# A decoder block with a mixture of experts: the two single pairs gathered row by row, filler products in the waits, and the closing stage written into both arms of the overflow branch

## The chip, the cores and the metric

The kernel runs on one core of a Trainium2 chip. The metric is the device time of one execution in microseconds (us), lower is better. The program is written by hand for five engines: TensorE (PE, matrix products, with its weight loads as PEld), VectorE (DVE), ScalarE (ACT), GpSimd (POOL) and SyncE (SP), whose queue here issues every transfer between the main memory and the on-chip memory SBUF. Products land in PSUM, which has eight banks of 128 x 512 float32.

## The reference

One layer on 512 tokens of width 1024, in float32: a first half (conditioned norm, one input projection, differential attention, a diagonal state-space branch, a gated merge) that leaves the residual `x`, and then a mixture of experts, which this document is about. Cut to its core, as the kernel computes it:

```python
h = modulate(rms_norm(x, norm2_g), shift2, scale2)            # 512 x 1024
grp = argmax(h @ w_rg + b_rg)                                  # one of 4 groups
top_v, top_i = top_k((h @ w_re + b_re)[grp], 2)                # 2 of the 8 experts in it
comb = p_grp * softmax(top_v)
for each token t and each of its two experts e:                # 32 experts in all
    a, g = split(h[t] @ w_e_in[e], 2)                          # 1024 -> 2 x 512
    moe[t] += comb * ((silu(a) * g) @ w_e_out[e])              # 512 -> 1024
x = x + gate2 * moe
y = rms_norm(x, final_g)
```

## The kernel before

The 32 experts are worked off as 16 pairs, p = 0 to 15 (`NP` = 16). An expert has 64 places (`CAP`), a pair has 128, so that one pair fills the 128 partitions. Four tiles of 128 tokens (`NT` = 4) feed the pairs. A token's row is brought to its place by a product with a selection matrix `P` (128 tokens by 128 places, a single 1 per chosen token; `P0` is that of pair 0, made during the routing). The normed input is kept as the sum of two tiles, `mh` + `ml`, so every such product is done twice.

For each pair, in order: `gather` (products at L1155) gives the transposed input `xT`, 1024 x 128, as eight blocks: for block k, tile i and half w the stationary operand is a 128 x 128 block of `mh` or `ml`, the moving one is `P`. Pairs are gathered two at a time (256 moving columns), except pair 0, gathered during the routing by `stage_x` (`x_` in the table `beside`), and pair 15, gathered alone when pair 13 is worked: both with 128 moving columns, 64 products each. Then `places` (L1341) finds token numbers and weights of the places, `hid_mm` (L1393) multiplies `xT` with `w_e_in` (tile `hid`), `act` and `act_turn` make and transpose the activated tile (`sa`, `xtp`, L1301), `yb_mm` (L1400) multiplies with `w_e_out` (tile `yb`), `weigh` weights it and splits it in two again (`yf`, `yh`, `yl`), and `give` (L1378) takes the rows back to the tokens with the transposed selection `PT` (tile `cb`), and adds them to `x` on DVE. `give` of pair p - 1 is done inside the pass of pair p.

The weights, 12 slots of 1 MB to a pair, stream through a ring of 17 slots. SP's queue issues them in order (`fetch`, L1263); each issue waits until the slot's last reader is done. The orders of PE and SP are written by hand in this part; DVE and ACT are ordered by a scheduler until pair 15's second half, and by hand from there on.

Ahead of the pairs stands the last product of the first half (`po`, L185), and between its steps the routing of the four token tiles, placed by the table `beside`: `t_` transposes, `l_` makes the logits (L1088) and ranks them on DVE, `h_` makes `mh` and `ml`, `r_` counts the places (L1137) and makes `P0` for one tile, `x_` gathers pair 0. After the last `po` of tile 3, step (3, 15), the rest of the routing has PE to itself.

At the end, after pair 15's first product, a register `ov` tells whether an expert got more than 64 tokens. Only then does `overflow` run, a long loop. The closing stage follows: pair 15's second product in five column pieces (`yq`, L1555), their way back to the tokens, and the final norm. In it GpSimd multiplies the left halves of `x` with `final_g` into the output tiles `fo`. In the profiled execution `overflow` did not run.

DVE's helpers have one line each for all their uses: L90 (`tt`, two tensors), L93 (`ts`), L96 (`stt`).

Of the kernel before, what the change touches and what calls it, by code (L numbers as in the profile page):

```python
# [19 lines left out]
T, D = 512, 1024  # L20
# [37 lines left out]
def hybrid_block(ctx: ExitStack, tc: tile.TileContext, x, cols, cst, ada_a, ada_b, b_rows, bc_rows, lamv, relb,  # L58
# [1098 lines left out]

    def weights():
# [49 lines left out]
    t_, l_, r_, h_, x_ = stage_t, stage_l, stage_r, stage_h, stage_x  # L1208
# [5 lines left out]
              (3, 15): [(x_, 1), (l_, 3, T, 256), (t_, 3, 768, 256), (r_, 2), (l_, 3, 768, 256), (h_, 3), (x_, 2), (r_, 3),  # L1214
                        (x_, 3)]}
    with tc.manual_schedule(engines={mybir.EngineType.PE}):
# [10 lines left out]
        for i in range(NT):  # L1227
# [11 lines left out]
            if i == 0:  # L1239
                xg0 = [bank(4 + q, (128, 4, 128), name="xg") for q in range(2)]  # L1240
# [81 lines left out]
    def gather(ps, P, h, between=None):  # L1322
# [121 lines left out]
    ctx.enter_context(tc.manual_schedule(engines={mybir.EngineType.SP, mybir.EngineType.PE}))  # L1444
    gate2 = per.tile([128, D], F32, tag="gate2", name="gate2")
# [6 lines left out]
    for h in range(2):  # L1452
        halves(x_half(0, h), xg0[h])
    for p in range(NP - 1):
# [73 lines left out]
    pl = [bank(4 + j, name="cb") for j in range(2)]  # L1528
    for j in range(2):
        give_mm(NP - 2, ys[1], 2 + j, pl[j])  # L1530
# [5 lines left out]
    for j in range(2):  # L1536
        add(2 + j, 512, pl[j])
# [5 lines left out]
    PIECES = ((0, 256), (256, 256), (512, 256), (768, 128), (896, 128))  # L1543
    fo = [slot("fo", free[0] + (3, 5, 8, 9)[i]) for i in range(NT)]
    yfs, yhl = slot("yf", free[0] + 6), slot("y", free[0] + 7, F32R)
    yp, ys, wide = {}, {}, {}
    nxf = nx.rearrange("p a b -> p (a b)")
    v4, y4, t4 = (nxf[:, 20 + 4 * j:24 + 4 * j] for j in range(3))

    def piece(q):  # L1550
        c0, n = PIECES[q]
        yp[q] = bank(q % 2, name="yq")[:, :n]
        for f in range(4):
            for e in range(2):
                TE.matmul(yp[q][64 * e:64 * e + 64], hT_[:, f, 64 * e:64 * e + 64], ring[NP - 1][8 + q][:, e, f],  # L1555
                          start=f == 0, stop=f == 3, skip_group_check=True)
        ys[q] = [yfs[:, 0, c0:c0 + n]]
        stt(ys[q][0], yp[q], disp[NP - 1][0][:, 6:7], gate2[:, c0:c0 + n], OP.mult, OP.mult)
        if q < 3:
            ys[q] += [yhl[:, j, c0:c0 + n] for j in range(2)]  # L1560
            S.copy(ys[q][1], ys[q][0])

    def second_part(q):
        yf, yh, yl = ys[q]
        tt(yl, yf, f32(yh), OP.subtract)
        ys[q] = [yh, yl]

    def to_tokens(qs_, i):
        for q in qs_:
            c0, n = PIECES[q]  # L1570
            if q < 2 and i == 0:
                wide[q] = pair(name="cb").rearrange("p a (b c) -> p (a b) c", c=256)
            elif q == 2:
                wide[2, i] = bank(4 + i, name="cb")
            give_mm(NP - 1, ys[q], i, wide[q][:, i] if q < 2 else wide[2, i][:, c0 - 512:c0 - 512 + n])

    def add_square(q, i):
        add(i, 256 * q, wide[q][:, i] if q < 2 else wide[2, i])
        square(q, i)

    def square(q, i):
        cs = slice(256 * q, 256 * q + (256 if q < 2 else 512))
        S.activation(fo[i][:, 1, cs], xs[i][:, cs], AF.Square, accum_out=nxf[:, 4 * q + i:4 * q + i + 1])

    def root(i):
        S.activation(t4[:, i:i + 1], nxf[:, 8 + i:9 + i], AF.Sqrt, bias=v4[:, i:i + 1], scale=1.0 / D)

    def inverse(i):

        v, y, t = (a[:, i:i + 1] for a in (v4, y4, t4))  # L1590
        emit(y, lambda: V.reciprocal(y, t))  # L1591
        stt(v, nxf[:, 8 + i:9 + i], 1.0 / D, v, OP.mult, OP.add)
        stt(t, y, -0.5, v, OP.mult, OP.mult)
        tt(t, t, y, OP.mult)
        stt(y, t, 1.5, y, OP.add, OP.mult)

    def finish(i):
        r_ = y4[:, i:i + 1]
        S.activation(fo[i][:, 0, :512], fo[i][:, 0, :512], AF.Copy, scale=r_)
        stt(fo[i][:, 0, 512:], xs[i][:, 512:], r_, fg[1], OP.mult, OP.mult)  # L1600
        nc.sync.dma_start(out[128 * i:128 * i + 128, :], fo[i][:, 0])

    def in_turns(*fs):
        for _ in in_steps([fs]):
            pass


    S.activation(t4[:, 0:1], eps6, AF.Sqrt)
    piece(0)
    second_part(0)  # L1610
    piece(1)
    for i in range(NT):
        to_tokens((0, ), i)
    for i in range(NT):
        add(i, 0, wide[0][:, i])
        if i == 1:
            second_part(1)
    for i in range(NT):
        square(0, i)
    piece(2)  # L1620
    for i in range(NT):
        to_tokens((1, ), i)
    for i in range(NT):
        add(i, 256, wide[1][:, i])
        if i == 0:
            second_part(2)
    for i in range(NT):
        square(1, i)
        tt(fo[i][:, 0, :512], xs[i][:, :512], fg[0], OP.mult, eng=G)
    piece(3)  # L1630
    piece(4)
    for i in range(NT):
        to_tokens((2, 3, 4), i)
        if i == 0:
            ts(v4, nxf[:, 0:4], 1.0 / D, OP.mult, 1e-6, OP.add)
            stt(v4, nxf[:, 4:8], 1.0 / D, v4, OP.mult, OP.add)
            add_square(2, 0)
            root(0)
        elif i < 3:
# [136 lines left out]
```

## Time and profile before

| what | value |
|---|---|
| median of 3 runs | 954.73 us (953.29 to 957.48) |
| the profiled execution | 954.63 us, of which its trace spans 952.5 us |
| PE busy | 909.0 us, 95% of the span |
| DVE, ACT, POOL busy | 501.5, 298.2, 7.2 us |
| mean granted clock of TensorE | 0.968 of full speed |
| weights and other transfers | 268.68 MB, mean 282 GB/s |

The profile's busy time of PE is no proof that PE does useful work at its full speed: products overlap, their ends are modelled, and the granted clock has two levels, 2.4 GHz (1.00 in the rows) and 1.2 GHz (0.50). The 2.1 us between the span and the execution's time lie outside the trace.

### The profile page before, as it was taken

How to read it: one execution, taken by the hardware profiler on the slowest of the kernel's cores; microseconds unless marked ns; L12 is line 12 of the kernel's file. 1: busy time of each engine (PE TensorE's matmuls, PEld its weight loads, DVE VectorE, ACT ScalarE, POOL GpSimd, SP SyncE). 2: the span in 40 equal slices, each digit the busy share in tenths (PEclk: the TensorE clock that was granted, in tenths of full speed). 3: DMA queues.
4: the chain of work that ended last, by engine and by line, in shares of the span. 5: the costliest groups of instructions: out<-in, count | busy, mean ns of one | idle time of the engine just before them, and what ended most of it. 6: DMA issues, size and time to landing. Idle time of an engine off the chain costs nothing. (4 is left out here: it accounts for less than half of the span.)

```text
span 952.5 us, 13019 instructions
## 1 busy us (share of the span) xinstructions
PE 909.0 (95%) x5028; PEld 569.9 (60%) x5028; DVE 501.5 (53%) x1249; ACT 298.2 (31%) x611; POOL 7.2 (1%) x12
## 2 busy tenths in 40 slices
PE   8997998889999999999999999999999999999985
PEld 4775765667777888779545554355553455546334
DVE  7896776656755566388315442244333343433336
ACT  3565578885544433242201010001010010100014
POOL 0000000000000000000000000000000000000002
PEclk9998998899999999998899999999999999997998
DMA  9925765512222633863799999999999999999902
GB/s 363 365 77 176 254 239 212 189 45 79 76 67 68 222 111 106 342 256 153 291 374 417 420 420 421 420 420 420 420 420 420 420 420 419 420 420 416 385 26 89
DMA packets 77589, 268.68 MB, mean 282 GB/s; under 512 B 5536, under 2 KB 11568, under 8 KB 77525
## 3 DMA queue, kind: packets, MB, share of 16 engines
q1 hardware_dynamic: 77524, 267.82, 71.6%
q8 instruction: 41, 0.67, 0.3%
q14 instruction: 24, 0.19, 0.1%
HBM read 265.68 MB, written 3.17 MB: 282 GB/s over the span
## 5 line engine op out<-in xcount | busy, mean ns | idle before, releaser
L1393 PE MATMUL hid<-w,xT 128*64 128x512 f32 x1024 | 225.7, 597 | 0.0
L1393 PEld LDWEIGHTS hid<-w,xT 128*64 128x64 f32 x1024 | 73.5, 138 | 146.8 <-issue 138.9
L1400 PE MATMUL yb<-w,sa 128*64 128x512 f32 x480 | 107.0, 598 | 0.0
L90 DVE TENSOR_TENSOR sa<-sa,hid 128x512 f32<-128x512 f32 (+1 forms) x17 | 11.1, 656 | 165.4 <-PE hid L1393 153.9
L90 DVE TENSOR_TENSOR wl<-ws,wh 128x1024 fp32r<-128x1024 f32 x52 | 63.4, 1221 | 54.8 <-ACT wh L153 44.1
L90 DVE TENSOR_TENSOR x<-x,cb 128x512 f32<-128x512 f32 (+1 forms) x132 | 80.2, 664 | 6.3 <-PE cb L1378 6.3
L153 ACT ACTIVATE wh<-ws 128x1024 fp32r<-128x1024 f32 x51 | 53.7, 1057 | 79.0 <-PE acc L180 24.8
L180 PE MATMUL acc<-hh,wh 128*128 128x512 f32 x176 | 74.1, 421 | 4.4 <-ACT wh L153 4.4
L1371 ACT CAST yh<-yf 128x512 fp32r<-128x512 f32 x29 | 17.9, 619 | 189.4 <-DVE yf L96 159.1
L1400 PEld LDWEIGHTS yb<-w,sa 128*64 128x64 f32 x480 | 33.4, 138 | 66.1 <-issue 66.1
L1155 PE MATMUL xg<-P,mh 128*128 128x256 f32 (+1 forms) x288 | 69.7, 294 | 1.5 <-DVE xT L1335 0.8
L180 PE MATMUL acc<-hl,wh 128*128 128x512 f32 x176 | 70.8, 403 | 0.0
L180 PE MATMUL acc<-hh,wl 128*128 128x512 f32 x176 | 70.6, 402 | 0.0
L1155 PE MATMUL xg<-P,ml 128*128 128x256 f32 (+1 forms) x288 | 68.7, 291 | 0.0
L1358 ACT ACTIVATE sa<-hid 128x512 f32<-128x512 f32 x15 | 9.0, 597 | 179.3 <-PE hid L1393 179.3
L96 DVE SCALAR_TENSOR_TENSOR yf<-yb,ws,gate 128x512 f32<-128x512 f32 x29 | 21.8, 751 | 82.2 <-PE yb L1400 81.8
L1155 PEld LDWEIGHTS xg<-P,mh 128*128 128x128 f32 x288 | 55.1, 201 | 2.2 <-DVE xT L1335 0.9
L1155 PEld LDWEIGHTS xg<-P,ml 128*128 128x128 f32 x288 | 55.4, 202 | 0.5
L1378 PE MATMUL cb<-yh,PT 128*128 128x512 f32 x116 | 49.3, 425 | 0.4 <-ACT yh L1371 0.3
L1378 PE MATMUL cb<-yl,PT 128*128 128x512 f32 x116 | 46.8, 404 | 2.2 <-DVE yl L90 2.0
L180 PEld LDWEIGHTS acc<-hh,wh 128*128 128x128 f32 x176 | 33.7, 191 | 14.1 <-ACT wh L153 4.6
L180 PEld LDWEIGHTS acc<-hh,wl 128*128 128x128 f32 x176 | 33.4, 190 | 9.4 <-issue 1.6
(304 smaller groups left out, 1424.0 us busy)
## 6 DMA issues: line engine op xcount, KB each, us to landing
w<-w_ein SPq DMA_DIRECT2D x128, 1024.0 KB, 13.7
w<-w_eout SPq DMA_DIRECT2D x63, 1024.0 KB, 17.4
ws<-units SPq DMA_DIRECT2D x52, 512.0 KB, 3.5
adaw<-ada_b SPq DMA_DIRECT2D x32, 512.0 KB, 4.6
ada<-ada_a SPq DMA_DIRECT2D x8, 512.0 KB, 8.2
ada<-ada_a SPq DMA_DIRECT2D x16, 256.0 KB, 7.3
X<-x SPq DMA_DIRECT2D x4, 512.0 KB, 6.3
x<-x SPq DMA_DIRECT2D x4, 512.0 KB, 4.9
```

The lines of the kernel that those rows point to most:

```text
L90: return emit(o, lambda: (eng or V).tensor_tensor(o, a, b, op=op))
L96: return emit(o, lambda: V.scalar_tensor_tensor(o, a, s, b, op0=op0, op1=op1, **k))
L153: return (lambda: S.activation(hi, st, AF.Copy) if u else V.tensor_copy(hi, st)), lambda: tt(lo, st, f32(hi), OP.subtract)
L180: TE.matmul(o, a, b, start=start and i == 0, stop=stop and i == 2)
L1155: TE.matmul(o, (h2h, h2l)[w][i][:, 128 * k:128 * k + 128], P[:, i].rearrange("p a b -> p (a b)"), start=start, stop=i == NT - 1 and w == 1 ...
L1358: S.activation(a, hid[0], AF.Silu)
L1371: S.copy(yh, yf)
L1378: TE.matmul(ps, PT if len(y) == 2 else f32(PT), a, start=w == 0, stop=w == len(y) - 1)
L1393: m = TE.matmul(hid[q][64 * e:64 * e + 64], xT[p, k // 4][:, k % 4, 64 * e:64 * e + 64], ring[p][k][:, e, 512 * q:512 * q + 512], start=k ...
L1400: TE.matmul(yb[q][64 * e:64 * e + 64], hT_[:, f, 64 * e:64 * e + 64], ring[p][8 + f][:, e, 512 * q:512 * q + 512], start=f == 0, stop=f == ...
```

## The change

Five things are changed, all in the second half of the program.

Single pairs: for pair 0 and pair 15 the operands change sides. `xr_mm` holds `P` of one tile stationary and moves 512 columns of `mh` or `ml`, so that a tile costs 4 products in place of 16. The result, `xr`, has the places as rows. It is copied to SBUF (`xrow`) and `turn_rows` transposes it with eight products (`xrt`) into `xT`, copied by DVE and ACT in halves.

Waits: `keep(n)`, in the table as `wm`, does n products of a tile of ones into a bank that nobody reads, 3 + 2 + 10 + 4 of them in step (3, 15).

Late scatter: the eight `give` of pair 14 stood in twos behind the steps of pair 15's `hid_mm`; now four stand behind the first step, two behind the last, and two behind the transposes `xtp`.

Closing stage: its code, now the function `ending`, stands twice: behind `overflow` in the one arm of the branch and by itself in the other, which comes first in memory. PE's hint on the branch is gone.

Last products: the four left halves are multiplied with `final_g` on DVE (`by_row`) and no longer on GpSimd.

```diff
+    def xr_mm(ps, P, i):
+        for w in range(2):
+            for q in range(2):
+                TE.matmul(ps[q], P[:, i].rearrange("p a b -> p (a b)"), (h2h, h2l)[w][i][:, 512 * q:512 * q + 512],
+                          start=i == w == 0, stop=i == NT - 1 and w == 1)
...
     def stage_x(i):
-        for w in range(2):
-            for k in range(KC):
-                xg_mm(xg0[k // 4][:, k % 4], P0, k, i, w, i == w == k % 4 == 0)
+        xr_mm(xr0, P0, i)
+    def keep(n):
+        ps = bank(0, name="wp")
+        for _ in range(n):
+            TE.matmul(ps, obf, obf[:, None, :].to_broadcast([128, 4, 128]), start=True, stop=True)
...
-              (3, 15): [(x_, 1), (l_, 3, T, 256), (t_, 3, 768, 256), (r_, 2), (l_, 3, 768, 256), (h_, 3), (x_, 2), (r_, 3),
-                        (x_, 3)]}
+              (3, 15): [(x_, 1), (wm, 3), (l_, 3, T, 256), (t_, 3, 768, 256), (r_, 2), (wm, 2), (l_, 3, 768, 256), (h_, 3), (x_, 2),
+                        (wm, 10), (r_, 3), (wm, 4), (x_, 3)]}
...
+    def turn_rows(p, rows, b):
+        for h in range(2):
+            tp = bank(b[h], (128, 4, 128), "xrt")
+            for k in range(4):
+                TE.transpose(tp[:, k], rows[:, 512 * h + 128 * k:512 * h + 128 * k + 128], ident)
+            halves(x_half(p, h), tp)
...
+    for h in range(2):
+        halves(xrow0[:, 512 * h:512 * h + 512], xr0[h])
+    turn_rows(0, xrow0, (7, 6))
...
         elif p == NP - 3:
             P = chosen(NP - 1, 1)
-            gather((NP - 1, ), P, 0, act_turned)
-            gather((NP - 1, ), P, 1)
+            xr = two(1, "xr")
+            for i in range(NT):
+                xr_mm(xr, P, i)
+                if i == 1:
+                    act_turned()
             places(NP - 1, P)
+            xrow = p2.tile([128, D], F32, tag="P", name="xrow")
+            for h in range(2):
+                (V.tensor_copy, S.copy)[h](xrow[:, 512 * h:512 * h + 512], xr[h])
...
+        if p == NP - 3:
+            turn_rows(NP - 1, xrow, (0, 1))
...
     for k in range(4, KC):
-        mm = hid_mm(NP - 1, hid, k)
+        hid_mm(NP - 1, hid, k)
         if k == 4:
-            with tc.issue_after(mm.ins):
-                tc.mark_branch_hint_location("overflow", "LikelyTaken", engines=[mybir.EngineType.PE])
-        if k < KC - 1:
-            for n in ((0, 1), (2, 3), (4, 5))[k - 4]:
-                give(NP - 2, ys[n // 4], n % 4, n // 4, 4 + n % 2)
+            for i in range(NT):
+                give(NP - 2, ys[0], i, 0, 4 + i)
...
-    with tc.If(ov > CAP, label="overflow"):
-        overflow()
+    def ending():
...
+        def by_row(i):
+            tt(fo[i][:, 0, :512], xs[i][:, :512], fg[0], OP.mult)
...
-        tt(fo[i][:, 0, :512], xs[i][:, :512], fg[0], OP.mult, eng=G)
...
+            if i < 2:
+                by_row(i)
...
+                by_row(i + 1)
...
+    with tc.If(ov > CAP, preferred_fallthrough_block=False) as fits:
+        overflow()
+        ending()
+    with fits.Else():
+        ending()
```

Three places of the engines' orders show what moved. The first is PE's order from the last logits of the routing to pair 0's `hid`, before:

```order
L1088 MATMUL lp_3597<-rwt,h2T 128x36 x2
L1155 MATMUL xg<-P_3596,mh 128x128 x8
L1155 MATMUL xg<-P_3596,ml 128x128 x8
L1137 LDWEIGHTS ubf
L1137 MATMUL lp_3597<-Ma,ubf 128x32
L1139 LDWEIGHTS obf
L1139 MATMUL lp_3597<-Ms_3588,obf 128x32
L1155 MATMUL xg<-P_3596,mh 128x128 x8
L1155 MATMUL xg<-P_3596,ml 128x128 x8
L1393 MATMUL hid<-w,xT 64x512 x32
```

The same place of PE now (`wp` is the filler's bank; its rows come ten times ahead of L1137 and four times behind L1139, and stand once each here):

```order
L1088 MATMUL lp_3597<-rwt,h2T 128x36 x2
L1162 MATMUL xr<-mh,P_3596 128x512 x2
L1162 MATMUL xr<-ml,P_3596 128x512 x2
L1216 LDWEIGHTS obf
L1216 MATMUL wp<-obf 128x512
...
L1137 MATMUL lp_3597<-Ma,ubf 128x32
...
L1139 MATMUL lp_3597<-Ms_3588,obf 128x32
...
L1162 MATMUL xr<-mh,P_3596 128x512 x2
L1162 MATMUL xr<-ml,P_3596 128x512 x2
L1353 MATMUL xrt<-colt,xrow 128x128 x8
L1412 MATMUL hid<-w,xT 64x512 x32
```

Sixteen narrow products became four wide ones at either place, fillers stand before and behind the count of places, and eight transposes now stand between the gather and `hid`.

The second place is PE at the end of pair 15's first product, before (`y` is one half of pair 14's weighted tile; the last row is the first of the closing stage, behind the code of `overflow`):

```order
L1393 MATMUL hid<-w,xT 64x512 x4
L1378 MATMUL cb<-y_7057,PT 128x512
L1378 MATMUL cb<-y_7058,PT 128x512
...
L1534 MATMUL xtp<-colt,sa 128x128 x4
L1539 TENSOR_LOAD ci
L1540 COMPARE_AND_BRANCH
...
L1540 UNCONDITIONAL_BRANCH
L1555 MATMUL yq<-w,hT 64x256 x16
```

The same place of PE now:

```order
L1412 MATMUL hid<-w,xT 64x512 x12
L1397 MATMUL cb<-y_7013,PT 128x512
L1397 MATMUL cb<-y_7014,PT 128x512
...
L1559 MATMUL xtp<-colt,sa 128x128 x4
L1397 MATMUL cb<-y_7013,PT 128x512
L1397 MATMUL cb<-y_7014,PT 128x512
...
L1566 TENSOR_LOAD ci
L1684 COMPARE_AND_BRANCH
L1581 MATMUL yq<-w,hT 64x256 x16
```

Three steps of `hid` now run without `cb` between them, two `give` stand behind the transposes, and `yq` follows the branch directly. The third place is DVE in the closing stage, as one piece of the difference:

```order
+L90 TENSOR_TENSOR fo<-x_0_3243,fg 128x512
 L93 TENSOR_SCALAR nx<-nx 128x4
 L96 SCALAR_TENSOR_TENSOR nx<-nx 128x4
 L90 TENSOR_TENSOR x_0_3243<-x_0_3243,cb 128x512
-L90 TENSOR_TENSOR x_1_3244<-x_1_3244,cb 128x512
-L90 TENSOR_TENSOR x_2_3245<-x_2_3245,cb 128x512
-L1591 RECIPROCAL nx<-nx 128x1
+L90 TENSOR_TENSOR fo<-x_1_3244,fg 128x512
+L90 TENSOR_TENSOR x_1_3244<-x_1_3244,cb 128x512
+L90 TENSOR_TENSOR fo<-x_2_3245,fg 128x512
+L90 TENSOR_TENSOR x_2_3245<-x_2_3245,cb 128x512
+L90 TENSOR_TENSOR fo<-x_3_3246,fg 128x512
```

Four products of 128 x 512 that GpSimd did are now between DVE's own, ahead of the first reciprocal.

## Rows read from the trace of the kernel before

**Rows 1.** Windows: stretch, length, busy us (instructions) of PE, PEld, DVE, ACT, POOL, PEclk, DMA share, GB/s.

```profile
460.00:850.00 390.00, 388.78 (x2037) 190.92 (x2035) 142.59 (x284) 33.58 (x66) 0.00 (x0) 1.00 1.02 415
454.00:459.00 5.00, 5.00 (x14) 1.61 (x15) 4.20 (x18) 3.20 (x6) 0.00 (x0) 0.51 0.02 8
908.00:924.80 16.80, 16.66 (x72) 6.37 (x68) 7.49 (x13) 1.83 (x3) 0.00 (x0) 1.00 0.00 1
```

**Rows 2.** Waits of PEld, 460 to 907: total us, times, longest.

```profile
PEld hid L1393 <- DMA w<-w_ein: 5.1, 18, 0.3
```

**Rows 3.** Timeline of PE, end of routing: start, length, line, tiles, [idle before, releaser].

```profile
445.46 1.95 PE L1155 MATMUL xg<-P,mh 128*128 128x128 f32 x8
...
449.76 0.19 PE L1137 MATMUL lp<-Ma,ubf 128*128 128x32 bf16 x1 [0.65 <-DVE Ma L96]
...
450.68 1.94 PE L1155 MATMUL xg<-P,mh 128*128 128x128 f32 x8 [0.70 <-DVE P L90]
...
454.25 16.23 PE L1393 MATMUL hid<-w,xT 128*64 128x512 f32 x64
```

**Rows 4.** Windows, as in the first group, of the two stretches at half clock.

```profile
445.40:458.90 13.50, 12.15 (x48) 8.73 (x49) 10.30 (x37) 4.34 (x8) 0.00 (x0) 0.50 0.64 258
861.60:871.60 10.00, 10.00 (x38) 8.00 (x39) 4.47 (x10) 0.00 (x0) 0.00 (x0) 0.50 1.02 419
```

**Rows 5.** Timeline of DVE, from the last P0 to pair 0's input.

```profile
450.24 0.29 DVE L90 TENSOR_TENSOR P<-cstt,Rm 128x128 fp32r<-128x128 f32 x1
450.45 1.28 DVE L90 TENSOR_TENSOR ml<-gate,mh 128x512 fp32r<-128x512 f32 x2
453.51 0.42 DVE L1295 COPY xT<-xg 128x256 f32<-128x256 f32 x1 [1.78 <-PE xg L1155]
```

**Rows 6.** Timeline of PE: pair 13 with pair 15's gather, then pair 14.

```profile
855.09 0.39 PE L1378 MATMUL cb<-yl,PT 128*128 128x512 f32 x1
855.32 0.22 PE L1155 MATMUL xg<-P,mh 128*128 128x128 f32 x1
...
857.06 0.62 PE L1301 MATMUL xtp<-colt,sa 128*128 128x128 f32 x4
...
877.99 13.90 PE L1393 MATMUL hid<-w,xT 128*64 128x512 f32 x64
...
896.35 0.50 PE L1378 MATMUL cb<-yl,PT 128*128 128x512 f32 x1 [1.40 <-DVE yl L90]
```

**Rows 7.** Timeline of PE, pair 15's hid to the closing stage.

```profile
918.30 1.94 PE L1393 MATMUL hid<-w,xT 128*64 128x512 f32 x8
...
921.30 1.94 PE L1393 MATMUL hid<-w,xT 128*64 128x512 f32 x8
...
924.20 0.60 PE L1534 MATMUL xtp<-colt,sa 128*128 128x128 f32 x4
928.33 3.67 PE L1555 MATMUL yq<-w,hT 128*64 128x256 f32 x32 [3.54 <-PEq L1540]
```

**Rows 8.** Instructions of L1540, the branch: queue, duration ns min/median/max, first and last start.

```profile
L1540 PEldq COMPARE_BRANCH  x1: 3110/3110/3110, 924.9 to 924.9; - x1
L1540 DVEq COMPARE_BRANCH  x1: 72/72/72, 925.4 to 925.4; - x1
```

**Rows 9.** Timelines of DVE and POOL in the closing stage.

```profile
938.50 0.98 DVE L93 TENSOR_SCALAR nx<-nx 128x4 f32<-128x4 f32 x1
939.59 1.11 DVE L96 SCALAR_TENSOR_TENSOR nx<-nx 128x4 f32<-128x4 f32 x1
940.62 1.87 DVE L90 TENSOR_TENSOR x<-x,cb 128x512 f32<-128x512 f32 x3
...
936.87 5.04 POOL L90 TENSOR_TENSOR fo<-x,fg 128x512 f32<-128x512 f32 x4 [905.48 <-DVE x L90]
```

**Rows 10.** Transfers of the output, L1601, from issue to landing.

```profile
DMA to landing us min/median/max: 2.6/2.6/2.6
```

**Rows 11.** Timeline of PE at the program's start: the filler that is there already.

```profile
1.07 9.82 PE L523 MATMUL wp<-obf 128*128 128x512 bf16 x36 [1.07 <-DVE obf L131]
```

More of the change, by code (lines that the diff above doesn't have):

```diff
@@ L1239, in hybrid_block @@
             if i == 0:
-                xg0 = [bank(4 + q, (128, 4, 128), name="xg") for q in range(2)]
+                xr0 = [bank(4 + q, name="xr") for q in range(2)]
+    xrow0 = per.tile([128, D], F32, tag="gate2", name="xrow")
     p1.close()
@@ L1544, in hybrid_block @@
[L1544 to L1575, printed above, removed]
@@ L1597, in finish @@
[L1597 to L1628, printed above, removed]
-        tt(fo[i][:, 0, :512], xs[i][:, :512], fg[0], OP.mult, eng=G)
[L1630 to L1639, printed above, removed]
-            add_square(2, i)
-            root(i)
@@ L1642, in hybrid_block, with piece, second_part, to_tokens @@
[L1642 to L1650 removed]
+    def ending():
+        PIECES = ((0, 256), (256, 256), (512, 256), (768, 128), (896, 128))
+        fo = [slot("fo", free[0] + (3, 5, 8, 9)[i]) for i in range(NT)]
+        yfs, yhl = slot("yf", free[0] + 6), slot("y", free[0] + 7, F32R)
+        yp, ys, wide = {}, {}, {}
+        nxf = nx.rearrange("p a b -> p (a b)")
+        v4, y4, t4 = (nxf[:, 20 + 4 * j:24 + 4 * j] for j in range(3))
+        def piece(q):
+            c0, n = PIECES[q]
+            yp[q] = bank(q % 2, name="yq")[:, :n]
+            for f in range(4):
+                for e in range(2):
+                    TE.matmul(yp[q][64 * e:64 * e + 64], hT_[:, f, 64 * e:64 * e + 64], ring[NP - 1][8 + q][:, e, f],
+                              start=f == 0, stop=f == 3, skip_group_check=True)
+            ys[q] = [yfs[:, 0, c0:c0 + n]]
+            stt(ys[q][0], yp[q], disp[NP - 1][0][:, 6:7], gate2[:, c0:c0 + n], OP.mult, OP.mult)
+            if q < 3:
+                ys[q] += [yhl[:, j, c0:c0 + n] for j in range(2)]
+                S.copy(ys[q][1], ys[q][0])
+        def second_part(q):
+            yf, yh, yl = ys[q]
+            tt(yl, yf, f32(yh), OP.subtract)
+            ys[q] = [yh, yl]
+        def to_tokens(qs_, i):
+            for q in qs_:
+                c0, n = PIECES[q]
+                if q < 2 and i == 0:
+                    wide[q] = pair(name="cb").rearrange("p a (b c) -> p (a b) c", c=256)
+                elif q == 2:
+                    wide[2, i] = bank(4 + i, name="cb")
+                give_mm(NP - 1, ys[q], i, wide[q][:, i] if q < 2 else wide[2, i][:, c0 - 512:c0 - 512 + n])
+        def add_square(q, i):
+            add(i, 256 * q, wide[q][:, i] if q < 2 else wide[2, i])
+            square(q, i)
+        def square(q, i):
+            cs = slice(256 * q, 256 * q + (256 if q < 2 else 512))
+            S.activation(fo[i][:, 1, cs], xs[i][:, cs], AF.Square, accum_out=nxf[:, 4 * q + i:4 * q + i + 1])
+        def by_row(i):
+            tt(fo[i][:, 0, :512], xs[i][:, :512], fg[0], OP.mult)
+        def root(i):
+            S.activation(t4[:, i:i + 1], nxf[:, 8 + i:9 + i], AF.Sqrt, bias=v4[:, i:i + 1], scale=1.0 / D)
+        def inverse(i):
+            v, y, t = (a[:, i:i + 1] for a in (v4, y4, t4))
+            emit(y, lambda: V.reciprocal(y, t))
+            stt(v, nxf[:, 8 + i:9 + i], 1.0 / D, v, OP.mult, OP.add)
+            stt(t, y, -0.5, v, OP.mult, OP.mult)
+            tt(t, t, y, OP.mult)
+            stt(y, t, 1.5, y, OP.add, OP.mult)
+        def finish(i):
+            r_ = y4[:, i:i + 1]
+            S.activation(fo[i][:, 0, :512], fo[i][:, 0, :512], AF.Copy, scale=r_)
+            stt(fo[i][:, 0, 512:], xs[i][:, 512:], r_, fg[1], OP.mult, OP.mult)
+            nc.sync.dma_start(out[128 * i:128 * i + 128, :], fo[i][:, 0])
+        def in_turns(*fs):
+            for _ in in_steps([fs]):
+                pass
+        S.activation(t4[:, 0:1], eps6, AF.Sqrt)
+        piece(0)
+        second_part(0)
+        piece(1)
+        for i in range(NT):
+            to_tokens((0, ), i)
+        for i in range(NT):
+            add(i, 0, wide[0][:, i])
+            if i == 1:
+                second_part(1)
+        for i in range(NT):
+            square(0, i)
+        piece(2)
+        for i in range(NT):
+            to_tokens((1, ), i)
+        for i in range(NT):
+            add(i, 256, wide[1][:, i])
+            if i == 0:
+                second_part(2)
+        for i in range(NT):
+            square(1, i)
+        piece(3)
+        piece(4)
+        for i in range(NT):
+            to_tokens((2, 3, 4), i)
+            if i < 2:
+                by_row(i)
+            if i == 0:
+                ts(v4, nxf[:, 0:4], 1.0 / D, OP.mult, 1e-6, OP.add)
+                stt(v4, nxf[:, 4:8], 1.0 / D, v4, OP.mult, OP.add)
+                add_square(2, 0)
+                root(0)
+            elif i < 3:
+                add_square(2, i)
+                root(i)
+                by_row(i + 1)
+        inverse(0)
+        finish(0)
+        in_turns(lambda: inverse(1), lambda: add(3, 512, wide[2, 3]))
+        square(2, 3)
+        root(3)
+        finish(1)
+        in_turns(lambda: inverse(2), lambda: inverse(3))
+        finish(2)
+        finish(3)
```

39 lines of the change are left out of this document (7 added, 32 removed).

## Prediction

> **What bounds it.** I read the windows first, the waits next, and then the timelines of PE and DVE around each edit. From 460 to 850 PE is busy for 388.78 of 390.00 us at full clock, so the pair passes end when PE ends; in the same stretch the transfers run at 415 GB/s with a busy share of 1.02, so PE and the weight stream are nearly balanced [rows 1]. Which of them is late? Weights wait for PE, by two rows: from 454 to 459 the transfers stand still (share 0.02, 8 GB/s), because the ring is full and PE has not freed a slot; and from 908.0 to 924.8 they stand still again, because all weights are in, while the last product that reads them starts only at 928.33 [rows 1, 7]. The weights thus finish some 20 us ahead of their last use. The waits of PE's weight loads on a transfer, 18 of at most 0.3 us and 5.1 us in all, come with no gap in PE [rows 1, 2]. A microsecond taken off PE anywhere behind 450 therefore reaches the end, until those 20 us are used up.
>
> Two stretches are slower than PE's own work: the granted clock is 0.50, the lower of two levels (1.2 GHz), for 13.5 us around the end of the routing and for 10.0 us in pair 13's pass [rows 4]. Both begin in or just behind runs of gather products with 128 moving columns, the kind that the change removes [rows 3, 6].
>
> **Pair 0's gather.** The place of the third tile is paced by DVE, not by PE: the count at 449.76 waits 0.65 us for `Ma`, `P` is made from 450.24 to 450.53, `ml` from 450.45 to 451.73 [rows 3, 5]. Up to there nothing is gained. Then 16 narrow products take 3.57 us at half clock, 450.68 to 454.25, and pair 0's `hid` 16.23 us, where a `hid` at full clock takes 13.90 [rows 3, 6]. After the change the last four wide products must wait for `ml` until about 451.8. A wide product at full clock is 0.23 us (the `cb` at 855.09 is followed by the next at 855.32) [rows 6]; the last one ends, with its latency of 0.39, near 452.1. Then come three short steps that overlap by halves: copy to SBUF 0.42 (as the copy at 453.51), four transposes about 0.4 (an estimate: 0.62 in the row at 857.06, less the pipeline's end of the last), copy 0.42 [rows 5, 6]. With hand-overs `hid` starts near 453.3: 0.95 us earlier. If the clock holds, `hid` gains 16.23 − 13.90 = 2.33 more. Together **−3.3 us**. Bounds: with wide products at half clock (0.43 by a full-width product's doubling, an estimate from 0.23) and the clock still low, the start gains 0.1 at best and `hid` nothing: 0; the other end is −3.8, if the hand-overs vanish.
>
> The 19 fillers: a filler of the same shape takes 9.82 / 36 = 0.27 us at the start of the program [rows 11]. The three and the two, 1.4 us, follow the gather of tile 1, which shortens from 16 narrow products (1.8 us at full clock, half of 3.57) to four wide ones (0.93), and lie in waits for DVE; the ten, 2.7 us, stand between 446.4 (the old 445.46 and four wide products) and the count at 449.76, which waits for DVE, so they end near 449.1; the four, 1.1 us, stand while `P` is made and delay the next product by at most 0.4, which `ml` hides. Zero, then. At half clock the ten would take some 5 us and push the count and all behind it by up to 1.5: this belongs to the first rival.
>
> **Pair 15's gather, in pair 13's pass.** From the first gather product at 855.32 to pair 14's `hid` at 877.99 there are 22.67 us: 64 narrow products, the transposes `xtp`, the product for the places, eight `cb` products and half of pair 13's `yb`, part of it at half clock [rows 4, 6]. After: 16 wide products 16 × 0.233 = 3.7 and two changes of kind 0.2, `xtp` 0.4, places 0.4, eight `cb` 2.0, eight transposes 0.9, `yb` at full clock 13.90 / 2 = 6.95: 14.5. The difference is **−8.2 us**. The copies of `xrow` (0.42 twice, DVE and ACT side by side) lie beside the eight `cb` products. Does `cb` now come too early for DVE? In pair 14, which has no gather, it waits 1.40 us for `yl` right behind `xtp`; here 3.9 us of products lie ahead of it, so no [rows 6]. Bounds: with 1.40 us of such waiting and the clock falling again for 10.0 us (5 us lost), −1.8; without hand-overs −8.5.
>
> **Late scatter and branch.** From 918.30 to 921.30, 3.00 us, stand eight `hid` products (13.90 / 8 = 1.74 in an unbroken run) and a burst of four `cb` products (4 × 0.233 = 0.93): 2.67 and 0.33 for the two changes of kind [rows 6, 7]. Four products now stand behind the transposes (0.93 less ahead of them), and of four bursts two are left, 0.33 less each: the transposes start at 922.6 instead of 924.20. Behind them PE ran into the branch: 3110 ns at 924.9, while DVE's took 72 ns; `yq` waited 3.54 us for PE's sequencer [rows 7, 8]. After the change the arm that runs stands next in memory. I take the branch at 0.07 to 0.4 with the four `cb` products (1.05) covering the copies of `hT`: 922.6 + 0.45 + 1.05 + 0.2 gives `yq` near 924.3 instead of 928.33: **−4.0 us**. Bounds: a branch of 3.11 again leaves −1.1, a free one gives −4.2. What is late next: DVE has four additions ahead of `yq`'s first weighting where it had two; they are done before `yq`'s first piece ends, or cost 0.25.
>
> The Trainium skill ("Runtime: NRT & Kernel Launch", section "Instruction fetch mechanics") says that an engine prefetches instructions in sequence only, and that a taken branch to code outside what it holds must fetch it first. The 3110 ns fit it, and no row here shows the fall-through. It also speaks against the change: the arm must now jump over `overflow` and the second copy of the ending, on every engine, at the very end.
>
> That jump at the end, by rows: PE and ACT take it early. SP and DVE take it with the last output in flight, which lands 2.6 us after its issue [rows 10]. A jump of 0.07 us is hidden; one of 3.11 sticks out by 0.5, and by 0.9 with the instructions behind it [rows 8, 10]. I take **+0.4**.
>
> **Last products.** GpSimd works from 936.87 to 941.91, and in that time DVE's two smallest instructions (128 x 4) take 0.98 and 1.11 us [rows 9]. Without GpSimd they should take no more than the 128 x 128 product at 450.24, 0.29 us each [rows 5]: 1.5 us freed, at most 2.1. Four products of 128 x 512 go onto DVE, at 1.87 / 3 = 0.62 us each [rows 9]: 2.5 us. With none of them in a wait of DVE the end comes 1.0 later, with one in a wait for `cb` 0.4, with two and 2.1 freed 0.8 earlier. I take **+0.6 us**, between the first two, since DVE is the later of the two engines there.
>
> **Sum.** −3.3 − 8.2 − 4.0 + 0.4 + 0.6 = −14.5. The profiled execution took 954.63 us, its median stands 0.1 higher at 954.73, so the sum goes over as it is: **940.1 us**. The lead of the weights, some 20 us, falls by the 11.5 us that PE gains in pairs 0 and 15, and by 4 in the tail. Against this the stream starts again sooner: it stands until 459 now, and the first slot comes free when the first eighth of pair 0's `hid` is done, after the change at 453.3 + 1.74 = 455.0, 4 us earlier [rows 1, 6]. The lead stays above 8 us; no wait for weights should appear.
>
> **Rivals.** *The clock falls in the routing all the same.* The stretch from 443 to 453 still waits for DVE several times, and fillers are only 19 × 0.27 = 5 us in it. For it: the fall at 445.4 came in a stretch with gaps [rows 3, 4]. Against: the second fall came with PE busy for all 10.0 us, so narrow products are enough and gaps not needed [rows 4]. Then pair 0's gain goes: −14.5 + 3.3 = −11.2, 943.5 us. *PE stalls at the fork again*, since it loads the register late or the code isn't there: −14.5 + 2.9, 943.1 us. The row of 3110 ns came with the closing code far off, which the change ends [rows 8]. *Weights become the bound.* The stream runs at 415 to 419 GB/s with its engines always busy [rows 1, 4]; if the lead of a middle pair is much below that of the last, PE's gain in pairs 0 and 15 is returned in waits for weights, and what is left is the earlier start of the stream (some 4) and the tail: about 947 us. Against it: the waits in [rows 2] are all short. If the stream doesn't start earlier either, only the tail is left, −3.4, and with an unseen wait in the ending the time is within 0.5%. *Slower:* the clock falls behind the new transposes, between wide products, and stays. Each us at half clock costs half a us, so it takes (14.5 + 4.8) × 2 = 39 us of half clock above today's 23.5 to end over 0.5% slower; a fall through some three passes would give about 960. The two falls seen lasted 13.5 and 10.0 us, which speaks against it [rows 4].
>
> **How the numbers follow.** Forecast 0.55; its own range is 937.2 (all terms at their better ends, −3.8 − 8.5 − 4.2 + 0 − 0.8 = −17.3) to 942.0 (jump 0.9, last products 1.0, 1 us of waits in pair 13). The others: clock in the routing 0.19; stall at the fork 0.10; weights bound with an earlier stream 0.07; no measurable change 0.05; slower 0.04. About 0.5%, 4.8 us, is what a measurement of this kernel can tell from no change. The first four are faster by more than that: 0.91. The range leaves out the last three cases, 0.16, on top and reaches 2.5 us above the two rivals at 943 for what they may have in common: up to 946. Below it goes to 936, the better ends less 1.2, about the distance of the median of before from its fastest run.
>
> **What would show it.** Right: PEclk 1.00 from 445 to 459 and through pair 13; pair 0's `hid` near 453.3 and 13.9 us long; some 14.5 us from the first `xr` of pair 15 to pair 14's `hid`; a branch of PE below 0.1 us and `yq` with no wait above 0.5; no POOL in the ending and DVE's `nx` below 0.3 us. Wrong: a `hid` that waits for `w` by more than 1 us, a filler behind which `Ma`'s count is late, or a jump at the end longer than 3 us.

## The result, and the profile after

The changed kernel takes 938.68 us (median of 4 runs, 938.26 to 938.94) against 954.01 us of the kernel before beside it (4 runs, 952.95 to 957.48): a ratio of 0.9839, 95% interval 0.9805 to 0.9873. The forecast was 940.1 in a range of 936.0 to 946.0. The profiled execution took 938.94 us, its span 937.1 (952.5 before).

Cut at the starts of instructions of PE (the last three rows: of `yq`, of DVE's first reciprocal, and the end), the two traces differ where the change is, and at one place more, the gather of tile 0:

| stretch of the trace | before | after | difference | forecast |
|---|---|---|---|---|
| start to pair 0's gather of tile 0 | 432.33 | 432.44 | +0.11 | 0 |
| to its gather of tile 1 | 9.40 | 8.53 | −0.87 | 0 |
| to the end of pair 0's `hid` | 28.69 | 25.39 | −3.30 | −3.3 |
| to pair 15's gather (13 passes) | 384.90 | 384.89 | −0.01 | 0 |
| pair 15's gather to pair 14's `hid` | 22.67 | 14.34 | −8.33 | −8.2 |
| to the second half of pair 15's `hid` | 33.95 | 33.94 | −0.01 | 0 |
| to `yq` | 16.39 | 12.08 | −4.31 | −4.0 |
| to the first reciprocal | 14.09 | 14.71 | +0.62 | +0.6 |
| to the end | 10.08 | 10.78 | +0.70 | +0.4 |
| sum | 952.5 | 937.1 | −15.4 | −14.5 |

The timeline of PE of the changed kernel at the end of the routing, and the granted clock there and around pair 15's gather (windows, columns as in [rows 1]):

```profile
440.97 0.63 PE L1162 MATMUL xr<-mh,P 128*128 128x512 f32 x2
...
445.40 2.33 PE L1216 MATMUL wp<-obf 128*128 128x512 bf16 x10
448.67 0.18 PE L1137 MATMUL lp<-Ma,ubf 128*128 128x32 bf16 x1 [0.93 <-DVE Ma L96]
...
450.11 1.07 PE L1162 MATMUL xr<-ml,P 128*128 128x512 f32 x2
451.09 1.45 PE L1353 MATMUL xrt<-colt,xrow 128*128 128x128 f32 x8
452.47 13.95 PE L1412 MATMUL hid<-w,xT 128*64 128x512 f32 x64
```

```profile
445.40:458.90 13.50, 12.46 (x59) 5.02 (x60) 11.55 (x42) 5.71 (x10) 0.00 (x0) 1.00 0.82 315
...
851.00:866.00 15.00, 15.00 (x76) 8.78 (x76) 7.64 (x18) 1.91 (x4) 0.00 (x0) 1.00 1.03 421
```

The clock is 1.00 in both places where it was 0.50 [rows 4]. The ten fillers end at 447.7, and the count behind them still waits 0.93 us for `Ma`: they cost nothing. `hid` takes 13.95 us and not 16.23 [rows 3].

PE around pair 15's gather and at the end of its `hid`:

```profile
851.25 0.63 PE L1162 MATMUL xr<-mh,P 128*128 128x512 f32 x2
...
857.70 1.04 PE L1353 MATMUL xrt<-colt,xrow 128*128 128x128 f32 x8
858.67 7.09 PE L1419 MATMUL yb<-w,sa 128*64 128x512 f32 x32
...
909.11 1.20 PE L1397 MATMUL cb<-y,PT 128*128 128x512 f32 x4
910.14 0.60 PE L1559 MATMUL xtp<-colt,sa 128*128 128x128 f32 x4
910.50 1.18 PE L1397 MATMUL cb<-y,PT 128*128 128x512 f32 x4
911.61 3.67 PE L1581 MATMUL yq<-w,hT 128*64 128x256 f32 x32
```

From `xr` to `yb` PE has no gap, and `yq` follows the last `give` without a wait. The branch, L1684, now comes twice on each queue, once at the fork and once at the end of the arm (queue, operation, duration in ns as min/median/max, starts):

```profile
L1684 SPq COMPARE_BRANCH  x2: 38/46/53, 899.3 to 933.0; - x2
L1684 PEldq COMPARE_BRANCH  x2: 95/1706/3317, 910.7 to 922.2; - x2
```

At the fork PE needs 95 ns; at the end of the arm 3317 ns, while its products run until 924.4 and nothing waits for it. DVE's timeline in the closing stage:

```profile
921.76 0.69 DVE L90 TENSOR_TENSOR fo<-x,fg 128x512 f32<-128x512 f32 x1
922.36 0.17 DVE L93 TENSOR_SCALAR nx<-nx 128x4 f32<-128x4 f32 x1
922.64 0.16 DVE L96 SCALAR_TENSOR_TENSOR nx<-nx 128x4 f32<-128x4 f32 x1
...
926.32 0.16 DVE L1621 RECIPROCAL nx<-nx 128x1 f32<-128x1 f32 x1
```

The two small instructions take 0.17 and 0.16 us where they took 0.98 and 1.11 beside GpSimd [rows 9].

### The profile page after: what moved, and what is told of

Read it like the earlier page. It is cut to its first block, busy times and chain, and to the rows that moved or that the text cites. A ratio compares the mean times of both kernels' runs of the same rounds, so it can differ in the third digit from the quotient of the medians.

```text
span 937.1 us, 12889 instructions
## 1 busy us (share of the span) xinstructions
PE 893.2 (95%) x4967; PEld 554.4 (59%) x4967; DVE 502.0 (54%) x1256; ACT 300.3 (32%) x616; POOL 2.2 (0%) x8
## 4 chain that ended last, share of the span: by engine, by line
PE 83%; ACT 6%; DVE 6%; DMA 3%; issue 1%; SPq 0%; DVEq 0%; ACTq 0%
PE hid L1412 23%; PE yb L1419 11%; PE acc L180 11%; PE cb L1397 7%; PE xg L1155 6%; PE pAS L180 5%; PE po L185 4%; PE acc L543 4%; DMA adaw<-ada_b 3%; ACT us L420 3%; PE plg L180 2%; ACT yf L698 2%; PE pv L864 1%; PE lp L1088 1%; PE mv L474 1%
## 5 line engine op out<-in xcount | busy, mean ns | idle before, releaser
L1412 PE MATMUL hid<-w,xT 128*64 128x512 f32 x1024 | 222.9, 592 | 0.0
L1155 PE MATMUL xg<-P,mh 128*128 128x256 f32 x224 | 54.7, 284 | 0.0
L1155 PE MATMUL xg<-P,ml 128*128 128x256 f32 x224 | 53.5, 280 | 0.0
L1155 PEld LDWEIGHTS xg<-P,ml 128*128 128x128 f32 x224 | 42.2, 189 | 0.5
L1155 PEld LDWEIGHTS xg<-P,mh 128*128 128x128 f32 x224 | 42.1, 188 | 0.5
```

The source lines that it names most:

```text
L1155: TE.matmul(o, (h2h, h2l)[w][i][:, 128 * k:128 * k + 128], P[:, i].rearrange("p a b -> p (a b)"), start=start, stop=i == NT - 1 and w == 1 ...
L1412: m = TE.matmul(hid[q][64 * e:64 * e + 64], xT[p, k // 4][:, k % 4, 64 * e:64 * e + 64], ring[p][k][:, e, 512 * q:512 * q + 512], start=k ...
```

## The experiments

Each is the changed kernel with one edit, unless it says otherwise. The part ahead of pair 0's gather of tile 1, where only the runs with narrow products for pair 0 differ in code, took a different time in each: that gather began between 439.97 and 443.93 us. Medians are therefore good for differences of some 4 us; smaller ones are read from stretches of the trace that begin behind that gather's start. Every kernel of the table has 4 to 10 runs.

| run | median us | ratio to before (95%) |
|---|---|---|
| no fillers | 943.03 | 0.9899 (0.9847 to 0.9951) |
| narrow products for pair 0, with fillers | 944.22 | 0.9905 (0.9875 to 0.9935) |
| narrow products for pair 15 | 946.98 | 0.9917 (0.9890 to 0.9944) |
| one branch, hint | 938.45 | 0.9852 (0.9800 to 0.9904) |
| one branch, no hint | 943.44 | 0.9869 (0.9824 to 0.9915) |
| before, closing stage in two arms | 952.63 | 0.9969 (0.9940 to 0.9999) |
| one branch, hint, old scatter | 939.82 | 0.9838 (0.9798 to 0.9879) |
| old scatter | 942.30 | 0.9881 (0.9840 to 0.9922) |
| last products on GpSimd | 938.79 | 0.9848 (0.9797 to 0.9899) |
| one branch, hint, GpSimd | 940.54 | 0.9844 (0.9805 to 0.9884) |
| last output on ScalarE's queue | 939.69 | 0.9854 (0.9813 to 0.9894) |
| half gather | 923.43 | 0.9687 (0.9644 to 0.9729) |

**What holds the clock in the routing.** Two runs complete a square of wide or narrow products with or without fillers. Without fillers:

```diff
-              (3, 15): [(x_, 1), (wm, 3), (l_, 3, T, 256), (t_, 3, 768, 256), (r_, 2), (wm, 2), (l_, 3, 768, 256), (h_, 3), (x_, 2),
-                        (wm, 10), (r_, 3), (wm, 4), (x_, 3)]}
+              (3, 15): [(x_, 1), (l_, 3, T, 256), (t_, 3, 768, 256), (r_, 2), (l_, 3, 768, 256), (h_, 3), (x_, 2),
+                        (r_, 3), (x_, 3)]}
```

> The changed kernel (938.7 us) without the 19 filler products of the routing; everything else stays. Theory: 128-column gather products alone brought the clock down, and the wide products that replaced them keep it up without help, so pair 0's hid still takes 13.9 us and starts near 452.5, and the time is 938.7 within 0.5. Rival: the fillers hold the clock over the waits for DVE; without them the granted clock is 0.50 again around 446 to 458, hid takes some 16 us, and the time is 941 to 942.

Its windows and PE's timeline:

```profile
447.00:448.00 1.00, 1.00 (x4) 0.82 (x4) 0.92 (x4) 0.02 (x1) 0.00 (x0) 0.59 1.01 414
446.00:452.00 6.00, 2.48 (x10) 1.66 (x10) 5.55 (x24) 1.60 (x3) 0.00 (x0) 0.60 1.01 407
452.00:459.00 7.00, 6.84 (x24) 3.59 (x26) 5.18 (x15) 2.99 (x6) 0.00 (x0) 0.61 0.52 211
```

```profile
443.38 0.63 PE L1162 MATMUL xr<-mh,P 128*128 128x512 f32 x2
...
445.55 0.41 PE L1082 MATMUL h2tp<-colt,gate 128*128 128x128 f32 x2 [0.71 <-DVE Ma L96]
...
446.42 0.64 PE L1088 MATMUL lp<-rwt,h2T 128*128 128x36 f32 x4 [0.42 <-ACT h2T L1084]
...
451.16 0.19 PE L1137 MATMUL lp<-Ma,ubf 128*128 128x32 bf16 x1 [2.48 <-DVE Ma L96]
...
456.10 14.58 PE L1412 MATMUL hid<-w,xT 128*64 128x512 f32 x64
```

The clock is at 0.50 from about 447.2 to 457.4, with wide gather products on both sides. Where the ten fillers stood PE waits 2.48 us, but the clock has fallen before that wait: what stands ahead of the fall are two shorter waits, 0.71 and 0.42 us, near the places of the three and the two fillers. Which of the 19 fillers are needed is thus not shown. From the gather of tile 1 to the end of `hid` this run takes 27.24 us against 25.39. The theory, narrow products alone, falls. The counterpart:

```diff
     def stage_x(i):
-        xr_mm(xr0, P0, i)
+        for w in range(2):
+            for k in range(KC):
+                xg_mm(xg0[k // 4][:, k % 4], P0, k, i, w, i == w == k % 4 == 0)
```

> The changed kernel with pair 0 gathered as before (four times 16 products of 128 columns, no rows, no transposes), but with the 19 fillers. With the run without fillers it makes a square: narrow and wide products, each with and without fillers. Theory that narrow products bring the clock down: 0.50 again from about 446, hid of 16.2 us, fillers take twice their time, 942 to 944 us. Rival, fillers hold the clock whatever the products are: hid 13.9 us, and only the length of the products is lost, 0.9 for tile 0 and up to 0.9 behind the last P0, less what the transposes cost: about 939.5 us.

```profile
446.53 1.11 PE L1155 MATMUL xg<-P,mh 128*128 128x128 f32 x8 [0.83 <-DVE P L90]
447.48 1.80 PE L1155 MATMUL xg<-P,ml 128*128 128x128 f32 x8
449.08 3.29 PE L1218 MATMUL wp<-obf 128*128 128x512 bf16 x10
452.20 0.18 PE L1137 MATMUL lp<-Ma,ubf 128*128 128x32 bf16 x1
452.42 1.02 PE L1218 MATMUL wp<-obf 128*128 128x512 bf16 x4
...
455.25 13.95 PE L1413 MATMUL hid<-w,xT 128*64 128x512 f32 x64
```

Here the clock falls too, at about 447.6, but is back at 1.00 by 451, within the fillers; `hid` has its 13.95 us. The ten fillers took 3.29 us for 2.33 and the count behind them no longer waits for DVE: PE is late. The stretch takes 27.82 us. So: narrow without fillers 28.69 (before), narrow with 27.82, wide without 27.24, wide with 25.39. The ends of this square repeat: all ten traces of kernels with wide products and fillers have 25.38 to 25.40 us, the two with neither 28.69 and 28.58; the mixed ones have one trace each. Neither half of the edit keeps the clock up by itself. The square isn't quite clean: with narrow products and fillers PE also waits 0.83 us for `P` ahead of the fall, which neither the kernel before nor the changed one does.

**Pair 15's gather.**

```diff
-            xr = two(1, "xr")
-            for i in range(NT):
-                xr_mm(xr, P, i)
-                if i == 1:
-                    act_turned()
+            gather((NP - 1, ), P, 0, act_turned)
+            gather((NP - 1, ), P, 1)
...
-        if p == NP - 3:
-            turn_rows(NP - 1, xrow, (0, 1))
```

> The changed kernel with pair 15 gathered as before (64 products of 128 columns in pair 13's pass, no row transposes). Theory: the term of 8.2 us comes back whole, of it about 5 by the clock at 0.50 for some 10 us and 3 by the products, their wait for the copy of xT and the longer order: 946.9 us. Rival: since PE is 12 us nearer to the weight stream there, part of the loss is hidden in slack of the transfers: 941 to 944.

From its first product (850.80) to pair 14's `hid` (873.46) there are 22.66 us, as before, against 14.34. The clock is at 0.50 again, from about 857 to 867, with PE busy throughout:

```profile
855.68 0.33 PE L1155 MATMUL xg<-P,mh 128*128 128x128 f32 x1 [0.78 <-DVE xT L1346]
```

```profile
860.00:870.00 10.00, 10.00 (x36) 6.13 (x37) 4.47 (x10) 0.00 (x0) 0.00 (x0) 0.64 1.02 419
```

The loss of 8.32 us is the theory's 8.2; no slack of the transfers hid any of it. But the narrow gather brings a wait as well: PE stands still for 0.78 us, until 855.68, for the copy of `xT`, some 1.2 us ahead of the fall, and for as long in the kernel before, until 860.20, some 1.5 us ahead of it. The change removes products and wait together, and no run parts them.

**The branch.** The closing stage behind the branch once more, with PE's hint:

```diff
+            with tc.issue_after(mm.ins):
+                tc.mark_branch_hint_location("overflow", "LikelyTaken", engines=[mybir.EngineType.PE])
...
-    with tc.If(ov > CAP, preferred_fallthrough_block=False) as fits:
+    with tc.If(ov > CAP, label="overflow"):
         overflow()
-        ending()
-    with fits.Else():
-        ending()
+    ending()
```

> The changed kernel with one copy of the closing stage, behind overflow, and PE's hint on the branch, as before. Theory: PE's branch takes 3.1 us again, of which the products now standing ahead of it hide little: yq starts 2.9 us later, and the end, where SP has no far jump, gains 0.7 us back: 940.9 us. Rival: the 3.1 us of the branch were covered by the copies of hT in part, and two give now cover more of it: 939.5 or less. If the 0.7 us at the end are not SP's jump, the time is 941.6.

```profile
L1686 PEldq COMPARE_BRANCH  x1: 403/403/403, 909.7 to 909.7; - x1
...
L1810 PEldq BRANCH_PREFETCH_HINT  x1: 41/41/41, 896.0 to 896.0; - x1
```

The branch jumps as in the kernel before and takes 403 ns, not 3110 [rows 8]. `yq` starts 1.84 us behind the transposes (1.47 with two arms), and from the transposes to the end it is 26.84 us (26.96). Both theory and rival missed the cause. I took the hint away:

> One copy of the closing stage behind overflow, as in the run with one branch, but without PE's hint. There PE's branch took 403 ns with the hint, and an instruction packet was moved between hint and branch. Theory: the hint had the closing code fetched; without it PE's branch takes some 3.1 us again, yq waits about 2.7 us longer, and the time from the transposes to the end grows from 26.8 to 29.5 us. Rival: where the code happens to lie decides, not the hint; the branch takes about 0.4 us again and the time is that of the run with the hint.

```profile
L1684 PEldq COMPARE_BRANCH  x1: 3484/3484/3484, 912.0 to 912.0; - x1
```

```profile
911.42 0.60 PE L1559 MATMUL xtp<-colt,sa 128*128 128x128 f32 x4
...
915.76 5.36 PE L1581 MATMUL yq<-w,hT 128*64 128x256 f32 x32 [2.81 <-PEq L1684]
```

So the hint does it. With the hint, a packet of the instruction queue q8 (taken for PE's, since in the kernel before its packet comes inside PE's branch) is moved between 899 and 900, some 3 us behind the hint; without it none between 895 and 912. In the kernel before, the hint ran too, at 909.4, 15.5 us ahead of the branch, and no packet of any kind was moved from 909 to 925; it came at 925 to 926, in the branch. The lines of the DMA view (queue, packets, MB, share of the engines), in the run with the hint for 896 to 900, and in the kernel before for 909 to 925 and for 925 to 926:

```profile
q8 instruction: 1, 0.02, 1.5%
```

```profile
DMA packets 0, 0.00 MB, mean 0 GB/s; under 512 B 0, under 2 KB 0, under 8 KB 0
```

```profile
q8 instruction: 1, 0.02, 5.9%
```

The stretch to the end is 30.78 us here, 1.3 above the 29.5 expected: behind the stall the clock is at 0.50 from about 916.5 to 919.9, and the first `yq` take 5.36 us instead of 3.67.

Was it the two `give` ahead of the branch, or something else that moved? One branch, the hint, and the old scatter:

```diff
-            for i in range(NT):
-                give(NP - 2, ys[0], i, 0, 4 + i)
+        if k < KC - 1:
+            for n in ((0, 1), (2, 3), (4, 5))[k - 4]:
+                give(NP - 2, ys[n // 4], n % 4, n // 4, 4 + n % 2)
```

> The changed kernel with the old end in both respects: one copy of the closing stage with PE's hint, and the eight late give in twos behind the steps of hid. From the kernel before it differs only in the gathers, the fillers and the products on DVE. Theory: the place of the code decides whether the hint helps, and it moved with the gathers: the branch takes about 0.4 us, and yq waits 0.5 us for hT. Rival: the two give between transposes and branch are what made the branch cheap; without them it takes 3.1 us and yq waits 3.5 us, as before.

```profile
L1685 PEldq COMPARE_BRANCH  x1: 412/412/412, 912.2 to 912.2; - x1
```

The branch is cheap with the old scatter too: the rival falls. (`yq` waits 0.82 us behind the transposes, put down to ScalarE's side of the branch, and not the 0.5 us for `hT` that were expected.) Nor is it the distance: the hint runs at 896.9 here, 15.3 us ahead of the branch, almost the 15.5 of the kernel before. What is left that differs from the kernel before is what stands earlier in PE's program (fewer gather products, fillers) and the closing stage's DVE part, which would fit the place of the code; no run moved the code alone. Why the hint moved nothing in the kernel before is not shown.

The two arms alone, in the kernel before:

> The kernel before with one change: the closing stage in both arms and no hint. Theory: PE's branch falls from 3110 ns to about 0.1 us; yq then waits about 0.5 us for the copies of hT, so it starts 3.0 us sooner after the transposes, and the end gives 0.7 back: 2.3 us faster from the transposes to the end (28.3 before). Rival: something else than the branch held yq, and it is below 1 us.

Transposes to end: 949.7 − 923.58 = 26.1 us against 28.3, 2.2 saved. PE's branch at the fork takes 95 ns and `yq` waits for the copies alone:

```profile
924.67 3.67 PE L1551 MATMUL yq<-w,hT 128*64 128x256 f32 x32 [0.49 <-DVE hT L1532]
```

**The late scatter** back, with two arms (the edit is that of the diff above, and the two `give` behind the transposes go):

> The changed kernel with the eight late give in twos behind the steps of hid, as before, and none behind the transposes. Theory: the transposes start 1.6 us later after hid's start; yq no longer has two give (1.05 us) ahead of it, but then waits for the copies of hT (about 0.5 us): yq 1.0 to 1.3 us later, 939.8 us. Rival: the change here only moved work from one side of the transposes to the other, 938.7 within 0.3.

From the second half of `hid` (901.55) to the transposes 12.26 us against 10.61, to `yq` 13.35 against 12.08: 1.27 us. In it `yq` waits 0.50 us for `hT`, the wait that the moved `give` cover:

```profile
914.90 3.67 PE L1579 MATMUL yq<-w,hT 128*64 128x256 f32 x32 [0.50 <-DVE hT L1560]
```

**The last products** on GpSimd again:

```diff
         def by_row(i):
-            tt(fo[i][:, 0, :512], xs[i][:, :512], fg[0], OP.mult)
+            tt(fo[i][:, 0, :512], xs[i][:, :512], fg[0], OP.mult, eng=G)
```

(and its four calls behind `square(1, i)`).

> The changed kernel with the four last products on GpSimd again, ahead of the last pieces. Theory: DVE saves 2.5 us of products and loses about 1.9 in its two 128 x 4 instructions that wait for GpSimd, so the first reciprocal comes 0.6 us sooner after yq: 938.1 us. Rival: the median follows the fewer microseconds of stalls instead, and it is 939 or more.

```profile
923.81 0.99 DVE L93 TENSOR_SCALAR nx<-nx 128x4 f32<-128x4 f32 x1
924.91 1.12 DVE L96 SCALAR_TENSOR_TENSOR nx<-nx 128x4 f32<-128x4 f32 x1
```

The slow pair is back, and the first reciprocal comes 14.09 us behind `yq`, not 14.71: this part of the change costs 0.62 us, as forecast. Both small differences together:

> The changed kernel with one copy of the closing stage and the hint, and the four last products on GpSimd. Theory: both small differences add, 0.1 from the one branch and 0.6 from the products: 26.2 us from the transposes to the end in place of 27.0, the median some 0.7 below that of the changed kernel on the same chip, which the spread of runs will hide. Rival: the code has moved again, the hint no longer helps, PE's branch takes 3.1 us and the stretch 29 us.

The branch takes 412 ns, and from the transposes to the end it is 936.9 − 910.68 = 26.2 us (26.96 with the change as made), as expected. The median, from another series of runs, can't tell this 0.7 us.

**The end of the arm.** 

```diff
-            nc.sync.dma_start(out[128 * i:128 * i + 128, :], fo[i][:, 0])
+            (nc.sync if i < 3 else nc.scalar).dma_start(out[128 * i:128 * i + 128, :], fo[i][:, 0])
```

> The changed kernel with the last of the four output transfers issued by ScalarE's queue and the other three by SP's. Theory: SP's jump at the end of the arm takes some 3 us and sticks out by 0.7 behind the landing of the last output; now SP jumps after its third issue, 0.8 us earlier, ACT's own jump is short, and the end comes 0.4 to 0.8 us sooner: 938.1 us. Rival: the end waits for the landing and the closing of all engines alone: 938.7 within 0.2.

From the first reciprocal to the end it is 10.82 us, as against 10.78: nothing gained, though SP's jump came 0.7 us sooner behind the reciprocal (6.0 for 6.7 us). But now ScalarE jumps last, behind its own issue:

```profile
L1684 ACTq COMPARE_BRANCH  x2: 38/44/49, 914.3 to 935.7; - x2
```

That is 6.4 us behind the reciprocal, so the last jump of all came only 0.3 us sooner. The trace of the changed kernel shows a packet of another instruction queue as late as 935 to 936, 2 to 3 us behind SP's jump at 933.0; the program's closing drains follow at 936.4. In this run that packet comes at 938 to 939, 2 to 3 us behind ScalarE's jump, and the drains at 939.3; both drains stand 10 us behind the reciprocal. Whether the packet stands behind the output's data or follows the last jump by a fixed time is not shown. That two arms cost 0.7 to 0.9 us at the end is shown: 10.02 to 10.08 us from the first reciprocal in the five kernels with one closing stage, 10.78 to 10.96 in the nine with two.

**How near the weights are.** The low parts of the gathers of pairs 1 to 14 are left out, so the values differ:

```diff
                 for i in range(NT):
-                    for w in range(2):
-                        xg_mm(xg[:, kk], P, 4 * h + k0 + kk, i, w, i == w == 0)
+                    xg_mm(xg[:, kk], P, 4 * h + k0 + kk, i, 0, i == 0)
```

> The changed kernel with the low parts (ml) left out of the gathers of pairs 1 to 14: 32 products of 256 columns fewer for every pair, about 3.7 us per gather of two pairs and half, 26 us of PE in all; the values change a little. It tells how near the weight stream is. Theory: the last weights land near 902 and are read up to 921, so about 17 to 18 us can be gained, and the rest turns into waits of hid and yb for w: 920 to 922 us. Rival: PE still bounds the passes: 912 to 913 us.

From pair 0's `hid` to `yq` it takes 441.75 us against 459.14, a gain of 17.4: the theory's number, but not by its cause. PE's busy time in the stretch falls by 22.6 us, from 456.3 to 433.7, and 5.2 us come back as new idle time. The largest wait of PE there has just this size, and is for an activated tile, not for weights:

```profile
PE ix L1359 <- DVE sa L1316: 5.2, 12, 0.5
```

The last packets of the weights come at about 903.4, and the last piece of `yq` that reads weights starts at 904.78, so 1.4 us of lead are left. In the changed kernel they come at about 903.8, and that piece starts at 919.47: 15.7 us.

## Why the prediction was right, step by step

**What bounds it.** Right. Thirteen pair passes between the changed places took 384.89 us after and 384.90 before, so what PE saved at 450 arrived whole. The weights' lead, counted as the prediction did up to the first piece of `yq`, fell from 19.3 us (909.0 to 928.33) to 7.8 (903.8 to 911.61): the 11.5 us that it allowed, ending just under its 8. The waits of weight loads on a transfer are as short as before, 23 of at most 0.3 us:

```profile
PEld hid L1412 <- DMA w<-w_ein: 6.6, 23, 0.3
```

**Pair 0's gather.** −3.30 for −3.3, with the split as forecast (start of `hid` 1.02 earlier behind the gather of tile 1, `hid` itself 2.28 shorter). Three things in it were wrong. The gather of tile 0 was left out of the sum: it stands among `po` products, PE-bound and at full clock, and gained 0.87 us; this is nearly all of the 0.9 that the sum missed. And the fillers were costed at zero and given no share in the gain; the square shows that wide products without them lose 1.85 of it. And the argument weighed against the first rival, that "narrow products are enough and gaps not needed", isn't shown: it counts PE as busy during the low clock, but 1.5 us ahead of that fall PE had waited 0.78 us, and without fillers the clock fell with no narrow gather product in the routing.

**Pair 15's gather.** −8.33 for −8.2, confirmed by its reversal, 8.32. Of it 5.3 us lie in the gather (its row transposes counted) and 3.0 in the products from there to pair 14's `hid`. What brought the clock down, the short products or the wait among them, stays open.

**Late scatter and branch.** −4.31 for −4.0. Scatter: 1.65 us less to the transposes (forecast 1.6), 1.27 to `yq` by its reversal alone. Branch: 95 ns, and the two arms alone give 2.2 net in the kernel before. But the step that the price goes away because the arm stands next in memory isn't the only way: with the gathers changed, the old form with its hint costs 403 ns, and the end 0.1 us less than two arms. In the changed kernel the two arms earn nothing that the hint would not have given.

The Trainium skill ("Runtime: NRT & Kernel Launch", section "Instruction fetch mechanics") has a taken branch to code that isn't held wait for a fetch. The packets agree: 3484 ns and a packet in the branch without the hint, 403 ns and a packet ahead of it with the hint.

**The jump at the end.** +0.70 for +0.4, inside its bounds of 0 to 0.9, but not as the bounds were reckoned: they took SP's branch at 0.07 to 3.11 us, and it took 53 ns at most. What the 0.70 us consist of is not shown, so here the number is right in part by luck. **Last products.** +0.62 for +0.6, with 1.76 us freed in DVE's two small instructions where 1.5 were taken.

**The range.** The better ends, −17.3 us, give 937.3 from the 954.63 of the profiled execution; the 937.2 of the prediction is a slip that changes nothing.

## What to carry to other kernels

A stretch in which one engine waits often, or runs many short products, should be read for the granted clock first: of the 3.30 us at pair 0, 2.28 were lost at 1.2 GHz in the `hid` that followed, and 3.0 of the 8.33 us at pair 15 in the products behind the gather. When a wait is priced from one trace, ask what else moves with the code: PE's branch cost 3.1 us in one program and 0.4 in another with the same source lines around it. And count all calls of a function that is edited, also those far from the place one looks at.

## What was not expected of the hardware

- A stall of PE at a branch (2.81 us) was followed, some 0.7 us into the next products, by 1.2 GHz for about 3.4 us: 5.36 us for 3.67. In the kernel before, a stall of 3.54 us wasn't; its `yq` took 3.67 [rows 7].
- GpSimd's 128 x 512 products held up DVE's instructions on 128 x 4 (0.98 and 1.11 us, again 0.99 and 1.12), but not its 128 x 512 additions, one operand of which lies in PSUM (1.87 us for three in all four kernels that have them beside GpSimd).
- A hint 13.7 us ahead of a branch moved an instruction packet, and the branch took 403 ns where it took 3484 without the hint; with the old scatter one 15.3 us ahead did the same (412 ns); one 15.5 us ahead in the kernel before moved none.
